# Low parts of the first mixer weights on VectorE, and another order for the first products of a decoder layer

## The chip, the core and the metric

The kernel runs on one core of one Trainium2 chip. Its engines work side by side and meet only through semaphores: TensorE (PE in the profile; PEld is its weight load, which runs beside the products), VectorE (DVE), ScalarE (ACT), GpSimd (POOL) and SyncE (SP), whose queue issues most of the DMA transfers. Each engine takes its own instructions strictly in their order in the program. An instruction that waits holds back everything behind it on its engine. The metric is the device time of one execution in microseconds (us), lower is better.

## The reference

One layer of a decoder trunk on one sequence of 1024 tokens with 1024 features, float32:

```
h = rmsnorm(x, norm1_w);  proj = h @ w_in
# mixer A: 4 heads of 128, gated delta rule in chunks of 64 after a causal convolution of width 4
qa, ka, va = silu(conv4(proj[q, k, v]));  qa, ka = l2norm(qa), l2norm(ka)
lmat = dec_strict * (kc @ kc.T) * beta             # per chunk and head, lower triangular
sol  = triangular_solve(lmat, [v, gam * k])        # unit diagonal
...                                                # a scan over the chunks carries the state
# mixer B: 8 heads of 64, three dilated causal windows, merged by their softmax denominators
x = x + concat(o_a, o_b) @ w_out
# MLP: 2816 wide, causal convolution of width 3 on both halves
u = conv3(rmsnorm(x, norm2_w) @ w_up);  x = x + (silu(gate) * up) @ w_down
out = rmsnorm(x, final_norm_w)
```

## The kernel before

**Products in three passes.** A float32 product is made of a high part and a low part of each operand. The high part `hi` is the value rounded to the format `fp32r` by a copy on ScalarE. The low part `lo` is the value less `hi`, made by one instruction with two inputs on VectorE (or GpSimd). A product of 128 rows by 512 columns then costs three matmuls, hi·hi, hi·lo and lo·hi (`mm3`). In the trace the high and low parts are called `xhi`, `xlo` (of the layer's input `xt`) and `whi`, `wlo` (of the weights `wst`, as they come by DMA).

**The start.** The input comes transposed as eight tiles `xt` of 128 features by 1024 tokens, the first one in two halves. A `split_x` makes its two parts, scaled by the norm's weights `n1`. The weights of the first keys (heads 0 to 2) come as four tiles `wst` of two feature blocks each, the first one in two pieces. Ahead of the real products TensorE runs 18 products of a tile of ones (`warm`), each a float32 matmul that shows as two rows in the trace. Then `first` works through the eight feature blocks: for each, six products (three heads by two halves of the tokens), three passes each, into six banks of PSUM (tags `hf`, `asc`, `ch`, two banks each). Beside it, ScalarE squares each `xt` (`sq`) and VectorE adds the squares up (`acc`), from which comes the norm's factor `rst` for each token (`rstdB` once it is spread out).

**The dense columns.** After that `dense` works through a list of 29 weight tiles, `DENSE`: the keys of head 3 (tile 0), the values of mixer B by token (tiles 1 to 8), queries and values of the four heads of mixer A (`q`, `v`, tiles 9 to 16), queries, keys of mixer B (`a`, tiles 17 to 24) and the gate `z` (tiles 25 to 28). `take` hands out a tile and prepares the next: `weight(..., spare=...)` makes `whi` on ScalarE, and `wlo` on VectorE, or on GpSimd where `spare` is true. There are two buffers each for `wst`, `whi` and `wlo`. A column's product goes to one of the two `hf` banks for each half of the tokens. VectorE reads the bank, scaled by `rstdB`, into `xr`, which frees it. For `q` and `v` follow the convolution (`qT`, `vT`: a copy on ScalarE, three instructions of 1023, 1022 and 1021 columns on VectorE, SiLU on ScalarE) and the transposes on TensorE (`ident,qT`, `ident,vT`) into the two banks `atr`. For `q` also the products with the keys (`qT,kT`), which VectorE reads as `at` out of the same `atr` banks.

**The triangular solve.** While the `q` and `v` columns run, VectorE solves the 32 by 32 triangular blocks of all chunks at once (`forward_sub`): 31 steps of two instructions, a product `tmp` of up to 256 elements for each partition and its subtraction from `xi`. The result goes through DRAM (`xdram`, `xtdram`) into the tiles `x64` and `um`, and TensorE merges the blocks (`merges`).

**What sets the order.** The program is written by generators that a small planner (`Weave`) interleaves: each one yields the time until it wants to go on, and the planner picks by an estimate of engine times. TensorE keeps the order in which the planner let the products be written. On the other engines the order follows the place in the program and priorities: `ve` and `ac` are VectorE and ScalarE at the usual priority (line 142 in the trace), `uv` and `ua` the same engines ahead of their turn (line 144). `after(inst, anchor)` forces one instruction behind another. Line 193 is a product, line 197 a transpose. `sy.dma_start` issues a transfer from SyncE, `sa.dma_start` from ScalarE's queue.

Of the kernel before, what the change touches and what calls it, by code (L numbers as in the profile page):

```python
# [7 lines left out]
F32 = mybir.dt.float32  # L8
F32R = mybir.dt.float32r
AF = mybir.ActivationFunctionType  # L10
OP = mybir.AluOpType
# [4 lines left out]
P = 128  # L16
S = 1024
KT = 8
# [129 lines left out]
def hybrid_layer(tc, I, out):  # L148
    nc = tc.nc
    wv = Weave()  # L150
    ve = Engine(wv, nc.vector, "vector", 0.07, 0.00105)
    ac = Engine(wv, nc.scalar, "scalar", 0.12, 0.00085)

    uv = Engine(wv, nc.vector, "vector", 0.07, 0.00105, first=tc.high_priority)
    ua = Engine(wv, nc.scalar, "scalar", 0.12, 0.00085, first=tc.high_priority)
# [33 lines left out]
    def after(inst, anchor, reason="keeps a slot free until it is needed"):  # L189
        tc.add_manual_dep(inst.ins, anchor.ins.name, order, reason=reason)  # L190

    def mm(dst, lhs, rhs, us, start=True, stop=True, **kw):
        tc.stamp_issue_order_token(nc.tensor.matmul(dst, lhs, rhs, start=start, stop=stop, **kw).ins, TOKEN)  # L193
        wv.product(us, dst, lhs, rhs)
# [44 lines left out]
    def wk(src, st=None):  # L239
        return [t.rearrange("p (k m) -> p k m", k=KT) for t in weight(src, st=st)]  # L240

    n1 = const("n1", [P, KT], I["n1"])
    mhalf = const("mhalf", [P, NCH])
    ve.memset(mhalf, -0.5)
    phalf = const("phalf", [P, NCH])
# [27 lines left out]
    def half(i):  # L273
        return slice(i * 512, i * 512 + 512)
# [7 lines left out]
    xs, xts = [], []  # L282
# [2 lines left out]

    def split_x(xt, k, sl):
        hi, lo = xs[k]
        ac.activation(hi[:, sl], xt[:, sl], AF.Copy, scale=n1[:, k:k + 1])
        ve.scalar_tensor_tensor(lo[:, sl], xt[:, sl], n1[:, k:k + 1], hi[:, sl].bitcast(F32), op0=OP.mult,
                                op1=OP.subtract)  # L290

    for k in range(KT):
        xt = A("xt", ("kT*", "dv*")[k % 2])
        xts.append(xt)
        if k % 2 == 0:
            wst = tile_(wp, [P, 2, 384], F32, "wst", "wst", 2)
            whi, wlo = [A(nm, "uy", F32R, (P, 2, 384)) if k < 4 else A(nm, "kt", F32R, (P, 2, 384))
                        for nm in ("whi", "wlo")]
            wk0.append((whi, wlo))
        xs.append((X("xhi"), X("xlo")))  # L300
        if k == 0:
            sy.dma_start(wst[:, 0, :], I["w0"][0, :, 0])
            for h in range(2):
                sy.dma_start(xt[:, half(h)], I["xT"][:P, half(h)])
            sy.dma_start(wst[:, 1, :], I["w0"][0, :, 1])
            split(wst[:, 0, :], whi[:, 0, :], wlo[:, 0, :])
            for h in range(2):
                split_x(xt, 0, half(h))
            split(wst[:, 1, :], whi[:, 1, :], wlo[:, 1, :])
        else:  # L310
            if k % 2 == 0:
                sy.dma_start(wst, I["w0"][k // 2])
            sy.dma_start(xt, I["xT"][k * P:(k + 1) * P, :])
            if k % 2 == 0:
                wlast = split(wst, whi, wlo)
            split_x(xt, k, slice(0, S))
        sq = A("sq", "qa")
        ac.activation(sq, xt, AF.Square)
        if k == 0:
            sq0 = sq  # L320
        elif k == 1:
            ve.tensor_tensor(acc, sq0, sq, op=OP.add)
        else:
            inst = ve.tensor_tensor(acc, acc, sq, op=OP.add)
            if k == 6:
                after(inst, first_lo, "the products wait for these weights")
        if k == 4:
            first_lo = wlast


    ident = const("ident", [P, P], I["ident"])
# [16 lines left out]


    wbank = bank("atr", "warm")  # L350
    for _ in range(18):
        mm(wbank[:, :P], warm, warm, 0.3)


    pst = [bank(t) for t in ("hf", "asc", "ch") for _ in range(2)]
# [1 line left out]
    def first():  # L357
        for k in range(KT):
            w = wk0[k // 2]
            for i in range(6) if k else (0, 2, 4, 1, 3, 5):  # L360
# [3 lines left out]
                mm3(pst[i], wm, [t[:, half(h)] for t in xs[k]], k == 0, k == KT - 1)  # L364
        wv.done.add("first")


# [1 line left out]
    rstdB = const("rstdB", [P, S])  # L369

    def norms():
        yield wv.need(acc, slack=8.0)
        ssp = yield from next_bank("atr", acc)
        for c in range(NCH):
            mm(ssp[:, c:c + 1], acc[:, c * P:(c + 1) * P], ones[:, :1], 0.215)
            if c % 2:
                yield APART
        ve.tensor_scalar(rst, ssp[:, :NCH], 1.0 / 1024, EPS, op0=OP.mult, op1=OP.add)
        rsqrt(rst, rst, NCH)
        wv.done.add("rst")  # L380
# [117 lines left out]
    def dense():  # L498
# [1158 lines left out]
```

## Time and profile before

| | |
|---|---|
| time, median of 3 runs | 1204.37 us (1203.77 to 1204.42) |
| time of the profiled execution | 1206.67 us |
| its span, from first to last instruction | 1204.6 us |
| TensorE busy | 1191.6 us (99%) |
| VectorE busy | 916.1 us (76%) |
| ScalarE busy | 575.3 us (48%) |
| GpSimd busy | 108.2 us (9%) |
| low parts of weights on GpSimd | 20 instructions, 47.9 us, 2393 ns each |

A row of the timeline gives the start, the length, the engine, the source line, the operation, what it writes and reads, its shape, how many instructions the row merges, and in brackets how long the engine had been idle before it and what it waited for. SPq marks the issue of a transfer from SyncE's queue. Lengths of matmuls run past the start of the next one, since they are pipelined: their rate is read from start to start. In the view by windows each engine's cell gives its busy time in the window and the number of instructions. PEclk is the granted share of TensorE's clock.

### The profile page before, as it was taken

Reading aid. Unit: us, or ns where it says so; the run is one execution under the profiler, and the core shown is the slowest. Engines: PE = TensorE matmul, PEld = TensorE weight load, DVE = VectorE, ACT = ScalarE, POOL = GpSimd, SP = SyncE. Lnnn points to the kernel's source line nnn. Section 1 sums busy time; section 2 is a strip of 40 time slices with the busy share of each in tenths; the row PEclk is TensorE's granted clock in tenths of the full one; section 3 lists DMA queues with packets and bytes.
Section 4 is the critical chain, followed back from the end, with each engine's and each line's share of the span. In section 5 each row is a group of like instructions: output and inputs, shape, how many; then the busy total and the mean of one; then the engine's idle time right before and its main releaser. Section 6 shows DMA issues by size and latency. Waiting matters only on the chain.

```text
span 1204.6 us, 18326 instructions
## 1 busy us (share of the span) xinstructions
PE 1191.6 (99%) x7068; PEld 987.0 (82%) x7068; DVE 916.1 (76%) x1442; ACT 575.3 (48%) x1126; POOL 108.2 (9%) x98
## 2 busy tenths in 40 slices
PE   9999999999999999999999999999999999999997
PEld 7888778889877778888888888888888888888886
DVE  7583985656365466767989989889898889999875
ACT  7375335456355443655545544444454454444441
POOL 0313232213422110000000000000000000000000
PEclk9999999999999999999999999999999999999998
DMA  7434233435624304444213122131322298547513
GB/s 235 107 93 121 103 109 119 149 115 164 222 94 128 95 36 120 169 140 140 84 56 106 58 100 91 67 105 53 105 73 85 94 370 305 180 162 226 165 54 140
DMA packets 85798, 154.80 MB, mean 129 GB/s; under 512 B 21168, under 2 KB 36304, under 8 KB 85712
## 3 DMA queue, kind: packets, MB, share of 16 engines
q1 hardware_dynamic: 85136, 153.12, 39.1%
q8 instruction: 55, 0.90, 0.3%
q10 hardware_dynamic: 576, 0.52, 0.1%
q14 instruction: 31, 0.25, 0.1%
HBM read 117.68 MB, written 35.93 MB: 128 GB/s over the span
## 4 chain that ended last, share of the span: by engine, by line
PE 93%; DVE 4%; ACT 1%; issue 1%; DMA 1%; SPq 0%; POOLq 0%; POOL 0%; DVEq 0%; ACTq 0%
PE ps L193 43%; PE pa L193 20%; PE dw L193 17%; PE pc L193 10%; PE ps L197 3%; DVE tmp L142 1%; DVE xi L142 1%; PE warm L193 1%; ACT sm L144 0%; DMA mt<-mdram 0%; DVE xr L142 0%; DVE qT L142 0%; DVE vT L142 0%; DMA mdram<-um 0%; DVE x1h L142 0%
## 5 line engine op out<-in xcount | busy, mean ns | idle before, releaser
L193 PE MATMUL dw<-pr 128*128 128x512 f32 (+1 forms) x984 | 211.3, 376 | 0.0
L193 PEld LDWEIGHTS dw<-pr 128*128 128x128 f32 x984 | 176.7, 188 | 33.6
L193 PE MATMUL ps<-xhi,whi 128*128 128x512 f32 x384 | 157.9, 411 | 0.5 <-DVE xr L142 0.5
L193 PE MATMUL ps<-xhi,wlo 128*128 128x512 f32 x384 | 150.5, 392 | 0.0
L193 PE MATMUL ps<-xlo,whi 128*128 128x512 f32 x384 | 150.3, 392 | 0.0
L193 PE MATMUL pa<-T,pair 128*128 128x512 f32 x528 | 127.0, 389 | 0.0
L193 PEld LDWEIGHTS pa<-T,pair 128*128 128x128 f32 x528 | 99.0, 188 | 20.6
L193 PEld LDWEIGHTS ps<-xhi,whi 128*128 128x128 f32 x384 | 72.7, 189 | 19.1 <-issue 5.6
L193 PEld LDWEIGHTS ps<-xhi,wlo 128*128 128x128 f32 x384 | 72.4, 188 | 15.8
L193 PEld LDWEIGHTS ps<-xlo,whi 128*128 128x128 f32 x384 | 72.7, 189 | 12.3
L142 ACT ACTIVATE u<-pa 128x512 f32<-128x512 f32 x44 | 26.3, 598 | 107.3 <-PE pa L193 107.3
L142 ACT ACTIVATE whi<-wst 128x1024 fp32r<-128x1024 f32 (+2 forms) x41 | 41.8, 1019 | 72.1 <-PE ps L193 40.3
L142 DVE SCALAR_TENSOR_TENSOR y<-xu,fcw,y 128x1023 f32<-128x1023 f32 (+1 forms) x44 | 56.4, 1281 | 22.1 <-ACT y L142 22.0
L142 POOL TENSOR_TENSOR rs<-rs,mhalf 128x2 f32<-128x2 f32 (+2 forms) x4 | 4.5, 1116 | 738.7 <-DVE rs L144 738.7
L193 PE MATMUL pc<-T,S 128*128 128x512 f32 x264 | 63.4, 389 | 0.0
L193 PE MATMUL pc<-B,pair 128*128 128x512 f32 x264 | 63.4, 389 | 0.0
L193 PE MATMUL pa<-B,A 128*128 128x512 f32 x264 | 63.4, 389 | 0.0
L193 PE MATMUL pa<-T,S 128*128 128x512 f32 x264 | 63.4, 389 | 0.0
L142 DVE TENSOR_TENSOR wst<-wst 128x512 f32<-128x512 f32 x88 | 60.5, 687 | 0.9
L193 PE MATMUL ps<-B,pair 128*128 128x512 f32 x252 | 60.5, 389 | 0.0
L144 ACT ACTIVATE sm<-sm,mx 128x128 f32<-128x128 f32 (+7 forms) x64 | 35.4, 555 | 47.9 <-DVE mx L144 47.9
L142 POOL TENSOR_TENSOR wlo<-wst,whi 128x1024 fp32r<-128x1024 f32 x20 | 47.9, 2393 | 115.6 <-ACT whi L142 113.7
(246 smaller groups left out, 2417.5 us busy)
## 6 DMA issues: line engine op xcount, KB each, us to landing
wst<-in_wu SPq DMA_DIRECT2D x44, 512.0 KB, 3.7
wd<-in_wd SPq DMA_DIRECT2D x44, 512.0 KB, 4.5
upark<-y SPq DMA_DIRECT2D x22, 512.0 KB, 3.7
wst<-in_wi SPq DMA_DIRECT2D x21, 512.0 KB, 3.7
r<-upark SPq DMA_DIRECT2D x11, 512.0 KB, 7.8
r<-upark SPq DMA_DIRECT2D x22, 256.0 KB, 6.8
wa<-in_wd SPq DMA_DIRECT2D x22, 256.0 KB, 3.1
wst<-in_wv SPq DMA_DIRECT2D x8, 512.0 KB, 3.7
```

What stands on the lines that cost most here:

```text
L142: return getattr(eng, op)(*a, **kw)
L144: return getattr(eng, op)(*a, **kw)
L193: tc.stamp_issue_order_token(nc.tensor.matmul(dst, lhs, rhs, start=start, stop=stop, **kw).ins, TOKEN)
L197: tc.stamp_issue_order_token(nc.tensor.transpose(dst, src, ident if idt is None else idt).ins, TOKEN)
```

## The change

1. `take` makes the low part on GpSimd only from tile 17 of `DENSE` on (before: from tile 9). So the eight tiles of the `q` and `v` columns of mixer A have their `wlo` made on VectorE.
2. The norm's weights `n1` and both pieces of the first weight tile are issued by ScalarE's queue; SyncE's queue begins with the two halves of the first `xt`.
3. TensorE runs 9 products of ones instead of 18.
4. For the first two feature blocks the products with the high part of the input (two passes) come first, and those with its low part behind them.
5. The splits of the first weights and of the input are ahead of their turn (`ua`, `uv`), and the squares and their sum are forced behind the splits of two blocks later.
6. The planner is told a longer notice for the norm's products (`slack=9.5`, before 8.0).

```diff
@@ take
-                nxt.append(weight(None, st=raw.pop(), spare=i >= 9))
+                nxt.append(weight(None, st=raw.pop(), spare=i >= 17))
@@ start
-    n1 = const("n1", [P, KT], I["n1"])
+    n1 = const("n1", [P, KT])
+    sa.dma_start(n1, I["n1"])
@@ split_x
-        ac.activation(hi[:, sl], xt[:, sl], AF.Copy, scale=n1[:, k:k + 1])
-        ve.scalar_tensor_tensor(lo[:, sl], xt[:, sl], n1[:, k:k + 1], hi[:, sl].bitcast(F32), op0=OP.mult,
-                                op1=OP.subtract)
+        inst = ua.activation(hi[:, sl], xt[:, sl], AF.Copy, scale=n1[:, k:k + 1])
+        if k == 0:
+            after(inst, his[0] if sl.start else whis[0], "in the order of arrival")
+        if k == 1:
+            after(inst, whis[1], "the weights come first")
+        his[k:] = [inst]
+        lo_of[0] = uv.scalar_tensor_tensor(lo[:, sl], xt[:, sl], n1[:, k:k + 1], hi[:, sl].bitcast(F32), op0=OP.mult,
+                                           op1=OP.subtract)
+    def split_first(src, hi, lo):
+        whis.append(ua.activation(hi, src, AF.Copy))
+        return uv.tensor_tensor(lo, src, hi.bitcast(F32), op=OP.subtract)
+    def square(k, hi, lo):
+        sq = A("sq", "qa")
+        late = "the products wait for the splits first"
+        after(ac.activation(sq, xts[k], AF.Square), hi, late)
+        sqs.append(sq)
+        if k == 1:
+            after(ve.tensor_tensor(acc, sqs[0], sq, op=OP.add), lo, late)
+        elif k > 1:
+            after(ve.tensor_tensor(acc, acc, sq, op=OP.add), lo, late)
@@ loop over the feature blocks
         if k == 0:
-            sy.dma_start(wst[:, 0, :], I["w0"][0, :, 0])
+            for j in range(2):
+                sa.dma_start(wst[:, j, :], I["w0"][0, :, j])
             for h in range(2):
                 sy.dma_start(xt[:, half(h)], I["xT"][:P, half(h)])
-            sy.dma_start(wst[:, 1, :], I["w0"][0, :, 1])
...
+        los.append(lo_of[0])
+        if k > 1:
+            square(k - 2, his[k], los[k])
+    for k in (KT - 2, KT - 1):
+        square(k, his[-1], los[-1])
@@ ones
-    for _ in range(18):
-        mm(wbank[:, :P], warm, warm, 0.3)
+    for _ in range(9):
+        mm(wbank[:, :P], warm, warm, 0.43)
@@ first
+            if k < 2:
+                for group in ((0, 2, 4), (1, 3, 5)) if k == 0 else (range(6),):
+                    for low in range(2):
+                        for i in group:
...
+                            if low:
+                                mm(pst[i], wm[0], lo, 0.2135, False, False)
+                            else:
+                                mm(pst[i], wm[0], hi, 0.2135, k == 0, False)
+                                mm(pst[i], wm[1], hi, 0.2135, False, False)
+                continue
@@ norms
-        yield wv.need(acc, slack=8.0)
+        yield wv.need(acc, slack=9.5)
```

The order of instructions on the engines moves at the start and around the `q` and `v` columns. ScalarE's first instructions (`n_72` is the tile of `n1`) were:

```order
L142 ACT_TABLE_LOAD
L142 ACTIVATE whi<-wst 128x384
L142 ACTIVATE xhi<-xt,n_72 128x512 x2
L142 ACTIVATE sq<-xt 128x1024
L142 ACTIVATE whi<-wst 128x384
L142 ACTIVATE xhi<-xt,n_72 128x1024
L142 ACTIVATE sq<-xt 128x1024
```

and are now:

```order
L142 DMA n_72<-in_n 128x8
L142 DMA wst<-in_w 128x384 x2
L144 ACT_TABLE_LOAD
L144 ACTIVATE whi<-wst 128x384
L144 ACTIVATE xhi<-xt,n_72 128x512 x2
L144 ACTIVATE whi<-wst 128x384
L144 ACTIVATE xhi<-xt,n_72 128x1024
L144 ACTIVATE whi<-wst 128x768
L144 ACTIVATE xhi<-xt,n_72 128x1024
L142 ACTIVATE sq<-xt 128x1024
```

Three issues of transfers stand ahead of the loading of ScalarE's function table, and the squares come later.

In the middle of the triangular solve, VectorE had in its queue, while the first `v` column ran:

```order
L142 TENSOR_TENSOR tmp<-mt,xi 128x231
L142 TENSOR_TENSOR xr<-ps,rstdB 128x512
L142 TENSOR_TENSOR xi<-xi,tmp 128x21x11
L142 TENSOR_TENSOR tmp<-mt,xi 128x240
L142 TENSOR_TENSOR xi<-xi,tmp 128x20x12
L142 SCALAR_TENSOR_TENSOR qT<-xr,gcw,qT 128x1023
L142 TENSOR_TENSOR tmp<-mt,xi 128x247
L142 SCALAR_TENSOR_TENSOR qT<-xr,gcw,qT 128x1022
L142 TENSOR_TENSOR xi<-xi,tmp 128x19x13
L142 SCALAR_TENSOR_TENSOR qT<-xr,gcw,qT 128x1021
L142 TENSOR_TENSOR xr<-ps,rstdB 128x512
```

and now has:

```order
L142 TENSOR_TENSOR xr<-ps,rstdB 128x512
L142 TENSOR_TENSOR tmp<-mt,xi 128x231
L142 TENSOR_TENSOR wlo<-wst,whi 128x1024
L142 TENSOR_TENSOR xi<-xi,tmp 128x21x11
L142 SCALAR_TENSOR_TENSOR qT<-xr,gcw,qT 128x1023
L142 TENSOR_TENSOR tmp<-mt,xi 128x240
L142 SCALAR_TENSOR_TENSOR qT<-xr,gcw,qT 128x1022
L142 TENSOR_TENSOR xi<-xi,tmp 128x20x12
L142 TENSOR_TENSOR xr<-ps,rstdB 128x512
L142 SCALAR_TENSOR_TENSOR qT<-xr,gcw,qT 128x1021
```

A `wlo` has come in, and the second `xr` (the first half of the `v` column) stands ahead of the last `qT` and of one step of the solve.

A little further, around the two reads `at` of the products of queries and keys, VectorE had:

```order
L142 SCALAR_TENSOR_TENSOR vT<-xr,gcw,vT 128x1021
L142 TENSOR_TENSOR tmp<-mt,xi 128x240
L142 TENSOR_TENSOR xr<-ps,rstdB 128x512
L142 TENSOR_TENSOR xi<-xi,tmp 128x12x20
L142 SCALAR_TENSOR_TENSOR at<-ps,bp,dec 128x128 x4
L142 SCALAR_TENSOR_TENSOR gq<-ngam,rq 128x8
L142 TENSOR_TENSOR tmp<-mt,xi 128x231
L142 TENSOR_TENSOR xi<-xi,tmp 128x11x21
L142 TENSOR_TENSOR tmp<-mt,xi 128x220
L142 SCALAR_TENSOR_TENSOR at<-ps,bp,dec 128x128 x4
```

and now has:

```order
L142 SCALAR_TENSOR_TENSOR vT<-xr,gcw,vT 128x1021
L142 TENSOR_TENSOR tmp<-mt,xi 128x252
L142 TENSOR_TENSOR xr<-ps,rstdB 128x512
L142 SCALAR_TENSOR_TENSOR at<-ps,bp,dec 128x128 x4
L142 SCALAR_TENSOR_TENSOR gq<-ngam,rq 128x8
L142 TENSOR_TENSOR xi<-xi,tmp 128x14x18
L142 TENSOR_TENSOR tmp<-mt,xi 128x247
L142 SCALAR_TENSOR_TENSOR at<-ps,bp,dec 128x128
L142 TENSOR_TENSOR xi<-xi,tmp 128x13x19
L142 SCALAR_TENSOR_TENSOR at<-ps,bp,dec 128x128 x3
```

The reads `at` now come at an earlier step of the solve. On TensorE the order of everything behind the norm's products is unchanged.

More of the change, by code (lines that the diff above doesn't have):

```diff
@@ L287, in split_x @@
         hi, lo = xs[k]
-        ac.activation(hi[:, sl], xt[:, sl], AF.Copy, scale=n1[:, k:k + 1])
-        ve.scalar_tensor_tensor(lo[:, sl], xt[:, sl], n1[:, k:k + 1], hi[:, sl].bitcast(F32), op0=OP.mult,
-                                op1=OP.subtract)
+        inst = ua.activation(hi[:, sl], xt[:, sl], AF.Copy, scale=n1[:, k:k + 1])
[9 more added lines that the diff above has]
+        return uv.tensor_tensor(lo, src, hi.bitcast(F32), op=OP.subtract)
+    his, los, lo_of, sqs, whis = [], [], [None], [], []
+    def square(k, hi, lo):
[7 more added lines that the diff above has]
+            after(ve.tensor_tensor(acc, acc, sq, op=OP.add), lo, late)
     for k in range(KT):
@@ L301, in hybrid_layer @@
         if k == 0:
-            sy.dma_start(wst[:, 0, :], I["w0"][0, :, 0])
+            for j in range(2):
+                sa.dma_start(wst[:, j, :], I["w0"][0, :, j])
             for h in range(2):
                 sy.dma_start(xt[:, half(h)], I["xT"][:P, half(h)])
-            sy.dma_start(wst[:, 1, :], I["w0"][0, :, 1])
-            split(wst[:, 0, :], whi[:, 0, :], wlo[:, 0, :])
+            split_first(wst[:, 0, :], whi[:, 0, :], wlo[:, 0, :])
             for h in range(2):
                 split_x(xt, 0, half(h))
-            split(wst[:, 1, :], whi[:, 1, :], wlo[:, 1, :])
+            split_first(wst[:, 1, :], whi[:, 1, :], wlo[:, 1, :])
         else:
@@ L314, in hybrid_layer @@
             if k % 2 == 0:
-                wlast = split(wst, whi, wlo)
+                split_first(wst, whi, wlo)
             split_x(xt, k, slice(0, S))
[L317 to L328, printed above, removed]
+        los.append(lo_of[0])
[3 more added lines that the diff above has]
+        square(k, his[-1], los[-1])
     ident = const("ident", [P, P], I["ident"])
@@ L359, in first @@
             w = wk0[k // 2]
-            for i in range(6) if k else (0, 2, 4, 1, 3, 5):
+            if k < 2:
+                for group in ((0, 2, 4), (1, 3, 5)) if k == 0 else (range(6),):
+                    for low in range(2):
+                        for i in group:
+                            m, h = divmod(i, 2)
+                            wm = [t[:, k % 2, m * P:(m + 1) * P] for t in w]
+                            hi, lo = [t[:, half(h)] for t in xs[k]]
+                            if low:
[4 more added lines that the diff above has]
+                continue
+            for i in range(6):
                 yield wv.need(*xs[k], *w)
@@ L363, in first @@
                 wm = [t[:, k % 2, m * P:(m + 1) * P] for t in w]
-                mm3(pst[i], wm, [t[:, half(h)] for t in xs[k]], k == 0, k == KT - 1)
+                mm3(pst[i], wm, [t[:, half(h)] for t in xs[k]], False, k == KT - 1)
         wv.done.add("first")
```

## The prediction

> **What bounds the kernel now.** I read the page first, then the windows of two stages, then the timeline of these.
>
> ```profile
> span 1204.6 us, 18326 instructions
> PE 1191.6 (99%) x7068; PEld 987.0 (82%) x7068; DVE 916.1 (76%) x1442; ACT 575.3 (48%) x1126; POOL 108.2 (9%) x98
> ...
> PE 93%; DVE 4%; ACT 1%; issue 1%; DMA 1%; SPq 0%; POOLq 0%; POOL 0%; DVEq 0%; ACTq 0%
> ```
>
> TensorE is the bound: it is busy 99% of the span and carries 93% of the chain that ended last. The amount of its real work does not change. So the time moves only where TensorE starts its real work late, waits, or runs at a lower clock. I looked for these places: the start, and a stage around 140 to 157 us.
>
> ```profile
> 1.10:6.70 5.60, 5.60 (x26) 5.60 (x27) 1.31 (x2) 2.15 (x3) 0.00 (x0) 1.00 0.74 202
> 6.70:7.80 1.10, 1.10 (x12) 1.10 (x11) 0.23 (x1) 0.99 (x2) 0.00 (x0) 1.00 1.00 340
> ...
> 150.00:153.50 3.50, 1.65 (x10) 0.94 (x8) 3.43 (x14) 0.04 (x1) 0.71 (x1) 1.00 0.00 0
> 153.50:157.00 3.50, 3.50 (x11) 2.92 (x12) 2.38 (x7) 2.43 (x9) 0.00 (x0) 0.51 0.37 150
> ```
>
> The cells after the window are TensorE, its weight loads, VectorE, ScalarE and GpSimd, then the granted clock. In the first window TensorE issues 26 rows of ones in 5.6 us (0.215 each), in the second 12 in 1.1 us (0.09). The clock's column says 1.00 in both, but the rate doubles at 6.7 us, so I go by the counts: half speed until then. From 153.5 on the clock itself is shown at 0.51 for 3.5 us, right behind a window in which TensorE was busy for only 1.65 us.
>
> **The start.** Here are the rows that lead to the first real product, and two of the norm's.
>
> ```profile
> 0.72 1.28 ACT L142 ACT_TABLE_LOAD   x1 [0.72 <-PEq L1649]
> 1.10 6.97 PE L193 MATMUL warm<-warm 128*128 128x128 f32 x36 [1.10 <-DVE ones L142]
> 1.18 0.41 SPq L142 DMA_DIRECT2D wst<-in_w  x1
> 1.64 0.90 SPq L142 DMA_DIRECT2D xt<-in_xT  x2
> 3.76 0.52 ACT L142 ACTIVATE whi<-wst 128x384 fp32r<-128x384 f32 x1 [1.76 <-DMA wst<-in_w]
> 4.57 0.72 ACT L142 ACTIVATE xhi<-xt,n 128x512 fp32r<-128x512 f32 x1 [0.28 <-DMA xt<-in_xT]
> 6.81 0.72 ACT L142 ACTIVATE xhi<-xt,n 128x512 fp32r<-128x512 f32 x1 [1.52 <-DMA xt<-in_xT]
> 7.83 0.48 PE L193 MATMUL ps<-xhi,whi 128*128 128x512 f32 x1
> 8.15 0.39 PE L193 MATMUL ps<-xlo,whi 128*128 128x512 f32 x1
> 8.38 0.39 PE L193 MATMUL ps<-xhi,wlo 128*128 128x512 f32 x1
> 26.96 1.22 DVE L142 TENSOR_TENSOR acc<-acc,sq 128x1024 f32<-128x1024 f32 x1
> 31.03 0.61 PE L193 MATMUL ps<-ones,acc 128*128 128x1 f32 x4
> ```
>
> The operands of the first product are there at 4.57 + 0.72 = 5.29, but TensorE is at its ones until 7.8. The second half of the input comes only at 6.81.
>
> *Half of the ones goes.* 18 rows at 0.215 from 1.10 end at 4.97 instead of 7.8.
>
> *The first transfers go to two queues.* The weights are again the second issue of their queue, so `wst` may land as now, at 3.76. The halves of `xt` are issued 0.9 us earlier each. ScalarE loads its table only behind three issues of about 0.41 us: from 0.72 to 1.95, and then 1.28 more, to 3.2. That is still ahead of 3.76, so it costs nothing as long as the landing takes that long. Then `whi` and `xhi` follow each other: 3.76 + 0.52 + 0.72 gives 5.0. The transfers of two queues overlap and may slow each other; 0.8 us (the first half of `xt` behind the weights, 4.57 less 3.76, is the nearest row) gives 5.8. I take 5.2, near the early end, because `xt` is issued earlier.
>
> *What these products cost before the clock rises.* From 5.2 to 6.7 they run at half speed, so 0.75 us of the gain is lost. The gain is 7.83 − 5.2 − 0.75 = 1.9 us, between 1.6 (start at 5.8) and 2.0 (start at 5.0). Putting the passes with `xhi` first lets `xlo` of each half come six products later; a pass takes 0.23 (8.15 to 8.38), so its cover is 1.4 us, and `xlo` on VectorE should take about as long as `xhi` on ScalarE, 0.72 (an estimate). With that order I see no wait behind the start.
>
> The Trainium skill speaks against this part in "DMA: Bandwidth & Descriptors", section "Issuing engines are not separate DMA queues": a second issuing engine saves only the time to issue, because all transfers run on the same 16 engines. By it the start is at the later end, 5.8, and the gain 1.6; no row of before shows two queues at once.
>
> *Squares and sums.* These move behind the splits, with the same count of instructions, so ScalarE and VectorE do the same work. Now the last sum ends at 28.2 and the norm's product runs at 31.03, 2.8 us later. In the new order one `wlo` more (1.1 us) stands ahead of the last sum, and the norm's product stands 12 passes (2.7 us) further on in TensorE's list, less the 1.9 us of the earlier start. So the cover stays at about 2.5 us, and I cost it at nothing, as I do the new `slack`.
>
> **The low parts on VectorE.** Here are TensorE's rows around its waits:
>
> ```profile
> 137.28 0.39 PE L193 MATMUL ps<-xhi,wlo 128*128 128x512 f32 x1
> 138.17 0.47 PE L193 MATMUL ps<-xhi,whi 128*128 128x512 f32 x1 [0.50 <-DVE xr L142]
> ...
> 139.40 0.39 PE L193 MATMUL ps<-xhi,wlo 128*128 128x512 f32 x1
> 139.91 1.09 PE L197 MATMUL ps<-ident,qT 128*128 128x128 f32 x8
> 140.76 0.48 PE L193 MATMUL ps<-xhi,whi 128*128 128x512 f32 x1
> ...
> 150.62 0.39 PE L193 MATMUL ps<-xhi,wlo 128*128 128x512 f32 x1
> 151.30 0.63 PE L197 MATMUL ps<-ident,vT 128*128 128x128 f32 x4 [0.29 <-DVE gq L142]
> 153.49 1.10 PE L197 MATMUL ps<-ident,vT 128*128 128x128 f32 x4 [1.56 <-DVE at L142]
> ```
>
> Taking 0.23 for a pass and 0.43 for four transposes (eight from 139.91 to 140.76), TensorE loses 0.66 at 138.17, 0.28 at 139.91, 0.45 at 151.30 and 1.76 at 153.49. Each time it waits for VectorE, or for ScalarE behind VectorE. And these are the rows that make VectorE late:
>
> ```profile
> 71.75 1.22 DVE L142 TENSOR_TENSOR wlo<-wst,whi 128x1024 fp32r<-128x1024 f32 x1
> 72.88 1.12 DVE L142 SCALAR_TENSOR_TENSOR um<-ps,bp,dec 128x128 f32<-128x128 f32 x4
> ...
> 127.64 2.53 POOL L142 TENSOR_TENSOR wlo<-wst,whi 128x1024 fp32r<-128x1024 f32 x1 [7.73 <-ACT whi L142]
> ...
> 127.95 2.46 DVE L142 TENSOR_TENSOR tmp<-mt,xi 128x220 f32<-128x220 f32 x1
> 130.45 0.39 DVE L142 TENSOR_TENSOR xi<-xi,tmp 128x220 f32<-128x220 f32 x1
> ...
> 136.15 1.27 DVE L142 SCALAR_TENSOR_TENSOR qT<-xr,gcw,qT 128x1021 f32<-128x1021 f32 x1
> 137.34 0.68 DVE L142 TENSOR_TENSOR xr<-ps,rstdB 128x512 f32<-128x512 f32 x1
> 137.50 1.28 ACT L142 ACT_TABLE_LOAD   x1 [4.44 <-DVE qT L142]
> 138.80 1.06 ACT L142 ACTIVATE qT<-qT 128x1024 f32<-128x1024 f32 x1
> ...
> 140.88 2.50 POOL L142 TENSOR_TENSOR wlo<-wst,whi 128x1024 fp32r<-128x1024 f32 x1 [10.71 <-ACT whi L142]
> ...
> 141.62 2.04 DVE L142 TENSOR_TENSOR xi<-xi,tmp 128x255 f32<-128x255 f32 x1
> 148.98 1.06 ACT L142 ACTIVATE vT<-vT 128x1024 f32<-128x1024 f32 x1 [4.03 <-DVE vT L142]
> 152.31 1.12 DVE L142 SCALAR_TENSOR_TENSOR at<-ps,bp,dec 128x128 f32<-128x128 f32 x4
> ```
>
> While GpSimd makes a `wlo` (127.64 to 130.17), an instruction of VectorE that usually takes 0.39 takes 2.46 and ends when GpSimd ends: 2.07 us lost. At 141.62 it is 2.04, so 1.64 lost. A `wlo` on VectorE itself costs 1.13 (71.75 to 72.88). So each moved `wlo` takes work off VectorE, and gives none to it on balance.
>
> *At 138.17 and 139.91.* Ahead of the `xr` that TensorE waits for, VectorE loses 2.07, gains 1.13, and has two steps of the solve (0.8) and the last `qT` (1.2) behind it instead of ahead: it ends at 138.02 − 2.9 = 135.1, while TensorE wants it at 137.5. The last `qT` ends 1.1 us earlier, so ScalarE's table and SiLU end at 138.75; TensorE, 0.66 earlier, wants it at 138.97. Both waits go: −0.9. The second has only 0.2 us of cover, so the bounds are −0.6 and −0.9.
>
> *At 151.30 and 153.49.* The second `at` ends at 153.43 now. Off it come 2.07 + 1.64, on it come two `wlo` (2.26), and five instructions of the solve (0.4 each, 2.0) that stood ahead now stand behind: 153.43 − 3.45 = 150.0. TensorE arrives at 153.49 − 0.94 − 0.45 − 1.76 = 150.3. Both waits go: −2.2, with bounds 0 and −2.2. All these times also move 1.9 us with the start, alike on every engine.
>
> *The clock.* Without these waits no window like 150.0 to 153.5 is left. So I take the stretch at 0.51 to go: 3.5 × 0.49 = −1.7, or 0 if a rest of the wait keeps it.
>
> *What the change queues up.* VectorE now waits for `whi` at the head of its queue, with the solve and `at` behind it. `whi` of that tile ends at about 139.8 by the earlier SiLU, when VectorE arrives. The solve ends about 3 us later than now, since the second `vT` stands ahead of its end; TensorE's first merges come much later in its list, so I cost that at nothing. SyncE's transfers of the next weights wait for VectorE instead of GpSimd, at about the same times.
>
> **The sum.** −1.9 − 0.9 − 2.2 − 1.7 = −6.7 us. The profiled execution took 1206.67 us around its span of 1204.6; the median of the runs is 1204.37, 0.2 below this span, so I take the sum off the median: 1197.7 us.
>
> **Rivals.**
>
> *A rest of the wait keeps the slow stretch.* If VectorE's second `at` comes 1 us later than worked out, TensorE waits 0.6 at 153.49, and with it the clock may fall as before. That gives 1197.7 + 0.6 + 1.7 = 1200.0. For it: the margin there is 0.3 us. Against: 1.65 busy of 3.5 is far from what would be left.
>
> *The clock rises one window later.* If TensorE stands idle between the ones and the first product, half speed may last one stretch of 3.5 us longer, which costs 1.75: 1199.4. For it: a start at 5.8 leaves 0.8 us idle behind the ones. The Trainium skill states this mechanism in "TensorE: Matmul & The Clock Gate", section "Part 1: The HAM clock gate (the "warmup" mystery)": half rate is the default, and only a free-running window of some 3.4 us that was busy lifts it, so ones that are taken away can hold it down. The stretch of 3.5 us at 0.51 agrees with it.
>
> *The long rows are not lost time.* If VectorE's 2 us beside GpSimd had another cause and stayed, the two `wlo` come on top. The second `at` would end at 153.43 + 2.26 − 2.0 = 153.7, TensorE would wait 3.4 there, the slow stretch would stay, and only the start and 0.9 would be won: 1204.4 − 2.8 + 1.2 = 1202.8. Against it stands that each long row ends with GpSimd's.
>
> *Slower: VectorE stands at the head of its queue.* If `whi` of the tile behind `tmp` 128x256 came only behind ScalarE's SiLU of `vT` (148.98 + 1.06, then 1.0 for itself: 151.0 instead of 139.8), VectorE would stand 11 us, and TensorE with it: 1197.7 + 10.9 = 1208.6. It decides from 7 us on. Against it: ScalarE's order there is the same as before.
>
> **How the numbers follow.** The forecast has 0.62, the rest of the wait 0.12, the later clock 0.13, the long rows that stay 0.07, the slower one 0.04, something unseen 0.02. 0.2% (2.4 us) is about what a measurement of this kernel can tell from no change. Faster holds the first three cases, 0.87; same the fourth and a part of the unseen, 0.08; slower 0.05. The range takes in the first three, 1196.7 to 1200.3; that of the forecast alone is 1196.9 to 1198.7.
>
> **What the profile after would show.** The first real product at about 5.2 us. No row of VectorE over 2 us between 120 and 200 us, and `wlo` rows of 1.2 there. No wait of TensorE over 0.3 us between 130 and 160 (in the times of now), and no window there at a clock of 0.51. The forecast is wrong if the first product starts after 6, if TensorE waits at `ident,vT` for `at`, or if a new wait stands at the merges.

## The result

| | before | changed |
|---|---|---|
| time, median of 11 runs | 1205.34 us (1203.77 to 1208.60) | 1201.77 us (1201.01 to 1203.01) |
| time of the profiled execution | 1206.67 us | 1201.61 us |
| its span | 1204.6 us | 1199.6 us |

The changed kernel takes 0.9973 of the time before, with a 95% interval of 0.9966 to 0.9981: 3.3 us less (2.3 to 4.1). It is faster, as forecast, but by half of the 6.7 us, and the time lies above the range. The two profiles are 5.0 us apart, more than the medians. So two questions stand: which terms of the sum did not arrive, and why do the profiles show more than the runs?

The first lines of the changed kernel's profile: TensorE is as busy as it was, and GpSimd has lost 21 us, most of it the eight low parts.

```profile
span 1199.6 us, 18291 instructions
PE 1186.8 (99%) x7050; PEld 983.1 (82%) x7050; DVE 915.6 (76%) x1450; ACT 574.8 (48%) x1126; POOL 87.2 (7%) x90
```

The view by windows, before, over the stage from 136 to 157 us (TensorE, its weight loads, VectorE, ScalarE and GpSimd, the granted clock, the DMA):

```profile
136.00:150.00 14.00, 13.37 (x71) 10.89 (x70) 13.72 (x23) 7.52 (x21) 4.72 (x2) 1.00 0.23 76
150.00:157.00 7.00, 5.15 (x20) 3.86 (x19) 5.81 (x20) 2.47 (x10) 0.71 (x1) 0.76 0.19 75
```

and the same windows of the changed kernel:

```profile
136.00:150.00 14.00, 14.00 (x76) 11.90 (x75) 13.56 (x31) 7.13 (x21) 1.75 (x1) 1.00 0.23 76
150.00:157.00 7.00, 7.00 (x37) 5.92 (x36) 6.42 (x13) 4.16 (x10) 0.00 (x0) 1.00 0.34 107
```

TensorE no longer waits there, and the clock stays up. The start also came earlier. But two other waits stand ahead of this stage. The changed kernel's timeline, on TensorE and on the engines that it waits for:

```profile
1.10 4.21 PE L193 MATMUL warm<-warm 128*128 128x128 f32 x18 [1.10 <-DVE ones L142]
...
5.01 0.52 ACT L144 ACTIVATE whi<-wst 128x384 fp32r<-128x384 f32 x1 [1.59 <-DMA wst<-in_w]
5.44 1.32 ACT L144 ACTIVATE xhi<-xt,n 128x512 fp32r<-128x512 f32 x2
...
6.20 0.50 PE L193 MATMUL ps<-xhi,whi 128*128 128x512 f32 x1 [0.88 <-ACT xhi L144]
...
8.19 0.53 ACT L144 ACTIVATE whi<-wst 128x384 fp32r<-128x384 f32 x1 [1.43 <-DMA wst<-in_w]
...
21.81 1.22 DVE L142 TENSOR_TENSOR acc<-acc,sq 128x1024 f32<-128x1024 f32 x1
...
23.08 0.95 DVE L144 TENSOR_TENSOR wlo<-wst,whi 128x768 fp32r<-128x768 f32 x1
...
24.09 0.50 PE L193 MATMUL ps<-xhi,wlo 128*128 128x512 f32 x1 [0.83 <-DVE wlo L144]
...
61.42 2.45 ACT L142 ACTIVATE dec<-dec,ngc 128x128 f32<-128x128 f32 x8 [1.37 <-DVE gel L142]
...
65.88 0.58 ACT L144 ACTIVATE ktok<-ps 128x512 f32<-128x512 f32 x1
...
67.52 1.16 PE L193 MATMUL ps<-kT 128*128 128x128 f32 x8 [0.61 <-ACT sq L144]
```

Before, the products `kT` (of the keys with themselves, for the triangular matrices) stood at:

```profile
67.29 1.16 PE L193 MATMUL ps<-kT 128*128 128x128 f32 x8
```

Following the same instruction of TensorE through both profiles gives the balance. The first product is 1.63 us earlier (7.83 to 6.20). Behind the wait at `wlo` 0.46 us are left (66.52 to 66.06, three passes ahead of `kT`). At `kT` TensorE is 0.23 us later (67.29 to 67.52): the start's gain is gone. At the transposes `ident,qT` it is 0.93 earlier (139.91 to 138.98), at the first `ident,vT` 1.44 (151.30 to 149.86), and behind the stretch at half clock 4.8. From there on little moves.

### The profile page after: what moved, and what is told of

Same layout as the page of the kernel before. It is cut to its first block, busy times and chain, and to the rows that moved or that the text cites. A ratio compares the mean times of both kernels' runs of the same rounds, so it can differ in the third digit from the quotient of the medians.

```text
span 1199.6 us, 18291 instructions
## 1 busy us (share of the span) xinstructions
PE 1186.8 (99%) x7050; PEld 983.1 (82%) x7050; DVE 915.6 (76%) x1450; ACT 574.8 (48%) x1126; POOL 87.2 (7%) x90
## 4 chain that ended last, share of the span: by engine, by line
PE 93%; DVE 2%; DMA 1%; ACT 1%; issue 1%; SPq 0%; POOLq 0%; POOL 0%; DVEq 0%; ACTq 0%
PE ps L193 44%; PE pa L193 20%; PE dw L193 17%; PE pc L193 10%; PE ps L197 3%; DVE kT L142 1%; DMA xt<-in_xT 1%; ACT sm L144 0%; DVE xr L142 0%; DMA alog<-in_a_log 0%; DMA n<-in_n 0%; DVE x1h L142 0%; PE pd L193 0%; DVE zz L142 0%; ACT dec L142 0%
## 5 line engine op out<-in xcount | busy, mean ns | idle before, releaser
L142 ACT ACTIVATE whi<-wst 128x1024 fp32r<-128x1024 f32 x36 | 38.3, 1063 | 67.8 <-PE ps L193 55.0
L142 ACT ACTIVATE pr<-wd 128x1024 fp32r<-128x1024 f32 x33 | 34.9, 1057 | 48.8 <-PE dw L193 38.9
```

Of the source, the lines that this page charges most:

```text
L142: return getattr(eng, op)(*a, **kw)
```

## Which part brought the time

Four kernels take the change apart. The first has only the new place of the low parts:

```diff
-                nxt.append(weight(None, st=raw.pop(), spare=i >= 9))
+                nxt.append(weight(None, st=raw.pop(), spare=i >= 17))
```

> The kernel before, and of the change only the low parts (GpSimd's from tile 17 on). Theory: the whole gain of the change comes from here: TensorE's waits at 138.17, 139.91, 151.30 and 153.49 and the stretch at half clock go, 0.9 + 2.2 + 1.7 = 4.8 us in the profile, so its span is 1199.8, as the changed kernel's within 0.3. Rival: the low parts bring less and the start brings the rest: the span is 1.5 us or more above the changed kernel's 1199.6.

Measured: 1201.91 us against 1205.23, ratio 0.9972 (0.9961 to 0.9983), span 1199.4. This is the changed kernel's time.

The second is the changed kernel with this one line undone (`i >= 9`), so that only the start differs from before.

> The changed kernel with GpSimd's low parts from tile 9 on, as before, so that only the start and its order are changed. Theory: the first product comes 1.6 us earlier (6.2), but TensorE waits about 0.9 us for `wlo` near 24 and 0.8 us at the products `kT` near 67.5, so nothing is left: the span is that of before, 1204.6, within 0.5 (and 0.2 above it by the two profiles' difference at 67.5). Rival: the waits near 24 and 67.5 came from the low parts' new place; then the span is 1.6 us below before.

Measured: 1205.18 us against 1205.23, ratio 0.9999 (0.9990 to 1.0008), span 1203.1. The first product stands at 6.37, and TensorE waits at both places, 0.5 and 0.4 us. The runs show no gain of the start in this program; the interval would leave room for about 1 us. (The span is 1.5 us under the first profile of before. The trace's record of the clock has no stretch at half clock in this execution, as in the second profile of before, below.)

The third is the changed kernel with the old number of ones:

```diff
-    for _ in range(9):
-        mm(wbank[:, :P], warm, warm, 0.43)
+    for _ in range(18):
+        mm(wbank[:, :P], warm, warm, 0.3)
```

> The changed kernel with 18 products of ones, as before, so that the first real product is held back to 7.8 us; all else as changed. Theory: TensorE then reaches `wlo` near 24 late enough not to wait there, and ends 0.6 us behind the changed kernel (1.6 later at the start, less the 0.94 that it no longer waits); if VectorE's chain alone sets the products `kT` at 67.5, even that goes, and the span is the same. So 1199.6 to 1200.3. Rival: the start's 1.6 us are a real gain that other parts hide: the span is 1201.2.

Measured: 1201.85 us, ratio 0.9970 (0.9960 to 0.9981), span 1200.3. The time doesn't move, as the theory has it. But the delay was smaller than I had written: the first product came at 6.89, not at 7.8, since the clock rose earlier in this execution (4.79 us) and the ones ran faster. TensorE still waited 0.4 us at `wlo` and 0.6 at `kT`; the theory had no wait at `wlo`.

The fourth is the kernel before, unchanged.

> The kernel before, once more, to see whether the stretch at half clock (153.5 to 157 us in its first profile, 1.7 us) belongs to every execution. Theory: it does, and the profile has a span of 1204.6 with a window at 0.5 right behind the wait for `at`. Rival: whether it comes depends on where the clock's windows happen to lie, so it is missing in some executions: a span near 1202.9 in those, and a spread of about 1.7 us between the executions. The rival would explain why the profiles of before and after lie 5.0 us apart, but the medians only 3.6.

Measured: 1205.23 us against 1205.23, ratio 1.0002 (0.9993 to 1.0011). Its profile has a span of 1202.6: 2 us under the first profile of the same program. Here are its windows, each 3.41 us long:

```profile
148.30:151.72 3.42, 3.06 (x17) 2.14 (x15) 3.36 (x11) 1.06 (x1) 2.13 (x1) 1.00 0.00 0
151.72:155.13 3.41, 1.92 (x11) 1.67 (x12) 3.23 (x11) 1.89 (x8) 0.00 (x0) 1.00 0.34 138
155.13:158.54 3.41, 3.41 (x17) 2.82 (x16) 3.34 (x5) 2.39 (x4) 2.10 (x1) 1.00 0.04 16
```

and those of the first profile of before:

```profile
150.13:153.54 3.41, 1.56 (x9) 0.85 (x8) 3.34 (x13) 0.01 (x1) 0.58 (x1) 1.00 0.00 0
153.54:156.96 3.42, 3.42 (x11) 2.84 (x12) 2.34 (x7) 2.38 (x9) 0.00 (x0) 0.50 0.38 153
```

I cut the windows so because the slow stretch is 3.41 us long, and because both the rise of the clock at the start (6.77 in the first profile, 4.96 in the second, by the trace's record of the granted clock) and the edges of this stretch fit a grid of that length: 6.77 + 43 × 3.413 = 153.53. Two waits of this stage are the same in both profiles, 1.6 us at `at` and 0.3 at `gq`. (The wait of 0.5 at `xr`, at 138.17, is in the first of the two alone.) In the first profile they fall into one window, TensorE is busy for 1.56 of 3.41 us, and the next window runs at half clock. In the second the grid divides them, TensorE is busy for 3.06 and 1.92 us, and the clock stays. So the stretch depends on where the grid lies when the program starts, and the rival is right: it isn't in every execution. The profile that I predicted from had it, and it was 1.3 us above the median of the runs. That is why the profiles differ by more than the medians. The Trainium skill, "TensorE: Matmul & The Clock Gate", section "Part 1: The HAM clock gate (the "warmup" mystery)", calls this window free-running, 3413 ns long; these rows agree. The runs give a hint of how many executions have the stretch. The first profile has a mean granted clock of 0.996, the second one 0.997. Of the 69 runs of before that were listed with a clock beside these experiments, 16 show 0.996, with a median span of 1204.4 us, and 27 show 0.998, with 1202.5. So about a quarter of the executions, or more, seems to have it; the 26 at 0.997 can't be assigned. Of the 19 runs of the changed kernel, two show 0.996 as well, so a slow stretch somewhere isn't ruled out there.

## What eats an earlier start

The view of waits on TensorE, from 8 to 200 us (what waited, for what, us in total, times, the longest), in the second profile of before:

```profile
PE ps L197 <- DVE at L142: 1.6, 1, 1.6
PE ps L193 <- ACT sq L144: 0.7, 1, 0.7
PE ps L197 <- DVE gq L142: 0.3, 1, 0.3
```

in the changed kernel:

```profile
PE ps L193 <- DVE wlo L144: 0.8, 1, 0.8
PE ps L193 <- ACT sq L144: 0.6, 1, 0.6
```

The wait for `sq` at the products `kT` belongs to the kernel before as well. It was missing in the profile that I read, where TensorE came 0.3 us later than in the second one (66.52 against 66.22, three passes ahead of `kT`) and ScalarE reached `ktok` 0.5 us earlier (65.66 against 66.17). The rows ahead of `kT` (above) show ScalarE at eight `dec` from 61.42, behind the copy `gel`, and only then at `ktok` and `sq`, whose bank the products `kT` want. Further ahead, VectorE's convolution of the keys doesn't take the same time in each execution, and GpSimd's four selections of `dec` run beside it (the last section has the rows). The same four instructions, before and in its second profile:

```profile
51.91 6.76 DVE L142 SCALAR_TENSOR_TENSOR kT<-xr,gcw,kT 128x1023 f32<-128x1023 f32 x4
```

```profile
51.60 7.59 DVE L142 SCALAR_TENSOR_TENSOR kT<-xr,gcw,kT 128x1023 f32<-128x1023 f32 x4
```

and the first of GpSimd's selections, in the second profile:

```profile
50.73 1.30 POOL L142 TENSOR_SCALAR_AFFINE_SELECT dec<-dec 128x1024 f32<-128x1024 f32 x1 [14.05 <-DMA dec<-gdram]
52.83 1.23 POOL L142 TENSOR_SCALAR_AFFINE_SELECT dec<-dec 128x1024 f32<-128x1024 f32 x1 [0.80 <-DMA dec<-gdram]
```

Four kernels test these waits. The first prepares the third tile of first weights earlier, so that its `wlo` no longer stands behind a sum:

```diff
@@ split_x
         if k == 1:
             after(inst, whis[1], "the weights come first")
+        if k == 6:
+            after(inst, whis[3], "the weights come first")
```

> The changed kernel, with the split of the third tile of first weights (feature blocks 4 and 5) forced ahead of the input's block 6 on ScalarE, so that its `wlo` is ready before TensorE wants it at 23.1 us. Theory: the wait of 0.94 us at 24.09 goes, but TensorE then waits that much longer for the bank of the products `kT` at 67.5, which ScalarE sets: the span stays at 1199.6 within 0.3. Rival: the two waits are separate losses: 1198.7.

Measured: 1201.42 us, ratio 0.9970 (0.9959 to 0.9982), span 1198.5. The wait at `wlo` is gone, and the one at `kT` did not grow (0.5). My theory missed this: VectorE's read `xr` ahead of the convolution waits for TensorE's product. It stands at 45.19 instead of 46.31, and TensorE itself is 1.12 us earlier there. So VectorE's chain moves along with TensorE, and the two waits are nearly separate losses. By the runs alone, 0.35 us isn't told from no change.

The second lets ScalarE's `dec` start earlier:

```diff
@@ conv_silu
             if j // 4 == 1 and d == 2 and klast:
                 after(inst, klast[-1], "the keys before go first")
+        if j == 4:
+            last["conv"] = inst
@@ kprep
-        after(ve.tensor_copy(gel, v8(dec)[:, :, P - 1]), kends[h][1], late)
+        after(ve.tensor_copy(gel, v8(dec)[:, :, P - 1]), kends[h][1] if h else last["conv"], late)
```

> The changed kernel, with VectorE's copy `gel` of head 0 right behind the convolution of these keys (59 us) instead of behind their last multiplication (61.2). ScalarE's eight `dec` can then start at 60.05 instead of 61.42, and its reads `ktok` and `sq` of the transposed keys, for which the products `kT` wait, at 64.95 (behind the `xr` that waits for VectorE until 63.9) instead of 65.88. Theory: this queue of ScalarE is what holds the products `kT` at 67.5; they come at 66.75 when TensorE arrives, and the span is 0.8 us shorter than the changed kernel's, 1198.8. Rival: VectorE's keys set it, and nothing moves: 1199.6.

Measured: 1201.55 us, ratio 0.9968 (0.9957 to 0.9980), span 1199.1. `ktok` comes at 64.47, and the products `kT` stand at 66.41 with no wait. So ScalarE's queue held them. (The four convolution instructions took 6.53 us in this execution and 7.36 in the changed kernel's, but that isn't the cause: the kernel with the start alone and the one with the early `wlo` had 6.52 and 6.53, and waited 0.4 and 0.5 us.) TensorE still waits 0.5 at `wlo`. By the runs alone, this kernel isn't told from the changed one either.

The third has both edits.

> Both of these edits together. Theory: TensorE arrives at the products `kT` at 65.8, and ScalarE has read their bank at about 64.95 + 1.64 = 66.6 (the distance from `ktok` to the products in the changed kernel), so 0.8 us of waiting are left and the span is 1198.7. Rival: the two edits add up: 1197.9.

Measured: 1200.02 us, ratio 0.9960 (0.9946 to 0.9973), span 1197.9. The span is the rival's figure: the two edits add up. Its timeline:

```profile
57.39 1.06 ACT L142 ACTIVATE xr<-kT 128x1024 f32<-128x1024 f32 x1 [5.35 <-DVE kT L142]
58.36 2.44 ACT L142 ACTIVATE dec<-dec,ngc 128x128 f32<-128x128 f32 x8
...
64.03 0.58 ACT L144 ACTIVATE ktok<-ps 128x512 f32<-128x512 f32 x1
...
65.97 1.05 PE L193 MATMUL ps<-kT 128*128 128x128 f32 x8
```

`dec` follows `xr` at once, where ScalarE stood idle for 1.37 us in the changed kernel, and between 8 and 200 us the view of waits of TensorE is empty.

The fourth moves one transfer:

```diff
@@ start
-    n1 = const("n1", [P, KT])
-    sa.dma_start(n1, I["n1"])
+    n1 = const("n1", [P, KT])
@@ loop over the feature blocks
-            for j in range(2):
-                sa.dma_start(wst[:, j, :], I["w0"][0, :, j])
+            sa.dma_start(wst[:, 0, :], I["w0"][0, :, 0])
+            sa.dma_start(n1, I["n1"])
+            sa.dma_start(wst[:, 1, :], I["w0"][0, :, 1])
```

> The changed kernel, with the first piece of the weights ahead of `n1` in ScalarE's queue. Theory on the landing: the transfers share the same engines, so the first piece, 0.45 us earlier in its queue, lands ahead of the second half of `xt` (about 4.2 instead of 5.0 us), and the first product starts near 5.4 instead of 6.2. Theory on the time: the 0.8 us of TensorE end in longer waits at `wlo` and at the products `kT`, and the span stays at 1199.6 within 0.3. Rival: the start counts, and the span is 1198.8.

Measured: 1201.09 us, ratio 0.9967 (0.9955 to 0.9979), span 1198.7. Its first splits:

```profile
4.44 0.52 ACT L144 ACTIVATE whi<-wst 128x384 fp32r<-128x384 f32 x1 [1.02 <-DMA wst<-in_w]
5.31 1.34 ACT L144 ACTIVATE xhi<-xt,n 128x512 fp32r<-128x512 f32 x2 [0.35 <-DMA n<-in_n]
...
7.38 0.53 ACT L144 ACTIVATE whi<-wst 128x384 fp32r<-128x384 f32 x1 [0.73 <-DMA wst<-in_w]
```

The weights landed earlier, but `xhi` then waited for `n1`, and the first product came at 6.09, only 0.1 us earlier. The span fell by 0.9 all the same, though the runs don't tell this kernel from the changed one. The second piece of the weights was split at 7.38 instead of 8.19, VectorE's chain of splits began that much earlier, and the view of waits shows none at `wlo`. In the six profiles with the new start and without the early `wlo`, this `wlo` starts 14.89 or 14.90 us behind the split of the second piece (8.19 to 23.08 in the changed kernel, 7.38 to 22.28 here). So the second piece sets when `wlo` is ready, the first product sets when TensorE wants it, and the wait near 24 is the difference. An earlier first product alone lengthens it.

## The start once the way is free

Four more runs follow. The first two are the changed kernel again, and the kernel with only the new low parts plus the early `gel` (so the old start).

> The changed kernel once more, beside the two that follow. Both theories: 1201.8 as before, waits near 24 (up to 1 us) and at the products `kT` (up to 0.8 us).

Measured: 1201.99 us, ratio 0.9974 (0.9964 to 0.9984), span 1199.3. TensorE waits 0.7 us at `kT` and not at all at `wlo`: the second piece of the weights was split at 7.83, and the first product came only at 6.74.

> The start of the kernel before, the low parts of the changed one, and the early copy `gel`. Theory: the products `kT` are what ate any earlier start, so with `gel` early the wait of 0.92 us there (that kernel without it) goes and the median falls from 1201.9 to about 1201.0. The old start brings the first product at 6.55, 6.97 or 7.83 in its three profiles, the new one at 6.1 to 6.5; so this kernel stays 0.5 to 1.0 us behind the one with the new start, the early `wlo` and the early `gel` (1200.0). Rival: the new start is worth nothing even then, and this kernel takes 1200.0 too.

Measured: 1201.14 us, ratio 0.9967 (0.9955 to 0.9979), span 1199.6, no wait at `kT`. But TensorE waited 0.7 us for an `xlo` at 12.15, so it came to `kT` 0.8 us later than in the kernel without the early `gel` (66.59 against 65.78, three passes ahead), and the profile doesn't show that `gel` alone removed the wait. With the new start and both edits the median was 1200.02, 1.1 us less. That points to the new start being worth about 1 us once nothing behind it takes it back, but the intervals of the two ratios overlap.

The next has the early `wlo`, the early `gel` and the moved `n1`.

> The changed kernel with the early `wlo`, the early `gel` and the first piece of weights ahead of `n1`. Theory: the first product starts at about 6.1 (its `xhi` waits for `n1`), 0.1 to 0.4 earlier than without the last edit, and no wait takes it back: 1199.7, about 2.1 us under the changed kernel. Rival: ScalarE's reads of the transposed keys take it back: 1200.0.

Measured: 1201.22 us, ratio 0.9965 (0.9952 to 0.9977), span 1199.3. Neither forecast: it is no faster than without the third edit. The timeline of the profiled execution shows a slow start:

```profile
1.10 4.21 PE L193 MATMUL warm<-warm 128*128 128x128 f32 x18 [1.10 <-DVE ones L142]
6.15 0.80 PE L193 MATMUL ps<-xhi,whi 128*128 128x512 f32 x1 [0.84 <-ACT xhi L144]
6.75 0.63 PE L193 MATMUL ps<-xhi,wlo 128*128 128x512 f32 x1
7.17 0.63 PE L193 MATMUL ps<-xhi,whi 128*128 128x512 f32 x1
```

The passes follow each other at 0.42 instead of 0.23: the clock rose only at 9.96 us. The window of the grid before that, and the one in which the changed kernel's clock was released:

```profile
3.13:6.55 3.42, 2.58 (x12) 2.29 (x11) 0.97 (x2) 1.98 (x4) 0.00 (x0) 1.00 1.04 387
```

```profile
2.42:5.83 3.41, 2.89 (x14) 2.60 (x13) 0.27 (x1) 1.82 (x3) 0.00 (x0) 1.00 1.01 330
```

TensorE was busy for 2.58 of 3.42 us there, and that was too little; 2.89 of 3.41 was enough. By this account the pause behind the nine ones made the difference, and where it falls in the grid is chance. So the last kernel has 13 products of ones in place of 9, and is otherwise the same:

```diff
-    for _ in range(9):
+    for _ in range(13):
         mm(wbank[:, :P], warm, warm, 0.43)
```

> The kernel with the three edits, with 13 products of ones instead of 9. In its profile with 9 the clock rose only at 9.96 us, and the first products, from 6.15 on, ran at half speed. Theory: the clock's window from 3.13 to 6.55 held too long a pause behind the ones (5.3 to 6.15), which depends on where the windows happen to lie; 13 products leave no such pause where the clock is still low, so the clock is up by 6.9 in the profile, and the median falls from 1201.2 to about 1199.8. Rival: the slow start is no matter of the ones; the clock rises as late again, and the median stays at 1201.2.

Measured: 1199.90 us (1199.70 to 1201.01) against 1205.51, ratio 0.9956 (0.9942 to 0.9970), span 1197.9. The clock rose at 6.02, the first product stands at 6.36, and TensorE has no wait between 8 and 200 us. This fits the theory but doesn't prove it: seven of the eight profiles with nine ones have an early rise too (4.04 to 5.83), and the intervals of the two ratios overlap. The runs lean the same way. With nine ones four of the five spans are 1199.3 us or more and one is 1197.5; with 13 four of five are 1198.1 or less. This is the fastest version, 1.9 us under the changed kernel's 1201.77. It isn't told from the one with two edits (1200.02).

## Why the prediction was wrong

The time is 4.1 us above the forecast (1201.77 against 1197.7). Of these, 1.0 comes from the reference: the median of before was 1204.37 in the three runs at hand and is 1205.34 in eleven. The start's 1.9 and the clock's 1.7 did not arrive in the median. The change as a whole brought 0.5 more than the 3.1 of the low parts.

**The low parts on VectorE: right.** The waits at 138.17, 139.91, 151.30 and 153.49 were put at 3.1 us, and all four went. The kernel with this part alone has the whole measured gain, 3.3 us. That the sizes fit so well is in part luck: the loss of 0.66 at 138.17 is missing in the second profile of before, and the 3.3 includes whatever the slow stretch is worth in the median. The rival that the long rows are no lost time is out. (A long row doesn't end exactly with GpSimd's, as the prediction has it, but 0.24 to 0.28 us behind it: 130.41 against 130.17, 143.66 against 143.38.) VectorE's solve in the changed kernel:

```profile
127.63 0.39 DVE L142 TENSOR_TENSOR tmp<-mt,xi 128x220 f32<-128x220 f32 x1
128.05 0.39 DVE L142 TENSOR_TENSOR xi<-xi,tmp 128x220 f32<-128x220 f32 x1
...
128.95 0.39 DVE L142 TENSOR_TENSOR tmp<-mt,xi 128x231 f32<-128x231 f32 x1
129.26 1.22 DVE L142 TENSOR_TENSOR wlo<-wst,whi 128x1024 fp32r<-128x1024 f32 x1
...
148.59 0.86 DVE L142 SCALAR_TENSOR_TENSOR at<-ps,bp,dec 128x128 f32<-128x128 f32 x3
```

No row is at 2.46 any more, `wlo` costs 1.13 (129.26 to 130.39), and the second `at` ends at 149.45, ahead of the forecast 150.0. The Trainium skill, "SBUF — State Buffer", section "Who interferes with whom", states this as a rule: a VectorE instruction with two inputs in SBUF and a GpSimd instruction that reads SBUF exclude each other. The row `tmp` 128x220 that went from 2.46 to 0.39 agrees.

**The start: the step that failed.** The prediction put −1.9 into the sum because the first product moves by that much. Three things were wrong with it.

- Its size: the first product came at 6.20, not at 5.2. The weights were split at 5.01, not at 3.76, although they were issued at the same time (1.17 and 1.18): they landed at 4.99, behind the two halves of `xt` at 3.53 and 4.77; before, they landed at 3.74, ahead of both. I had kept the old landing, and 5.8 for the late end was too early as well. The Trainium skill's rule in "DMA: Bandwidth & Descriptors", section "Issuing engines are not separate DMA queues", pointed to the later end, and the trace agrees with it. On the other hand the clock was already up (5.83), so nothing was lost at half speed, and the first product's gain in the profile was 1.63. That it still lies between the 1.6 and 2.0 of the prediction is luck: two errors cancel.
- Its reference: how early the old start is depends on when the clock lets the 18 ones pass. With the old start the first product came at 7.83, 6.97, 6.55 and 6.83 in four profiles; I had read the latest. With the new start it came at 6.20, 6.74 and 6.37 in three, and at 6.19, 6.12 and 6.54 in three more that differ from it only later. By these means the gain is 0.6 to 0.7 us.
- Its way to the end: "with that order I see no wait behind the start". VectorE's sums and splits run from 9 to 24 us almost without a gap, and they did not become earlier: the third tile's `wlo`, at 22.89 before, stands at 23.08, while TensorE wants it 1.6 us earlier than before. The wait there took 0.9 us, and ScalarE's queue at `kT` took what was left. A wait of zero in the trace of before was taken for a margin; it was none.

**The clock: right in the profile, wrong in the sum.** The stretch at half clock went from the profile, with 1.6 us. But it belonged to that one execution, and was taken off the median of the runs. The prediction set that median, 1204.37, beside the span, 1204.6, and saw 0.2 us between them. The time of the same execution was 1206.67, 2.3 us above the median of then and 1.3 above that of eleven runs.

**The rivals.** "The clock rises one window later" was given 0.13. Neither profile of the changed kernel has it, but it is real: the profile of the kernel with three edits shows it, and its windows fit the mechanism that was named. No VectorE stall at the head of its queue was seen.

## What to carry over

An earlier start is worth only what every join behind it lets through: before counting it, look at each place where TensorE meets another engine, and ask how much earlier that engine will be, not whether it waits now. A loss that hangs on the clock's windows belongs to one execution; hold the profile's own time against the median before such a term goes into the sum. And a cheap test for a part that "must" help is to run it alone, or to undo it alone.

## What the runs showed of the hardware

The clock's windows keep one grid of 3.41 us through the execution, and its place differs from one execution to the next. In all 14 profiles the time from the clock's rise at the start to its fall at the end, by the trace's record, is a whole number of windows of 3.413 us: 1187.84 us or 348 windows in the changed kernel's, 347 to 349 in the others. In mid-kernel, a window in which TensorE was busy for 1.56 of 3.41 us was followed by one at half clock, one with 1.92 was not. At the start a window with 2.58 us did not release the clock, one with 2.89 did. The busy time of the profile isn't the whole measure, though: at the end of the kernel with 18 ones the window from 1189.21 us has 2.61 us, some of it products of a single column, and half clock follows from 1192.63.

GpSimd's selections slow VectorE as its low parts do, and what counts is which of the two starts first. Each of the 14 profiles has five convolution instructions of these keys near 50 to 59 us. The 36 that start while a selection runs take 1.51 to 2.13 us. Of the other 34, two start within 0.04 us ahead of a selection and take 2.18 and 2.20; 32 take 1.27 to 1.28, also where a selection starts soon behind them (53.34 and 53.57 us in the first profile of before; that selection takes 1.99, one that nothing holds up 1.09). So the same four instructions took 6.76 us in one execution of before and 7.59 in another.
